# One decoder layer on one core: sums of W_down made in DRAM early, sums of x made on z between products

## The chip, the cores and the metric

The kernel runs on one core of one Trainium2 chip. The core has five engines that run their own instruction streams: TensorE (PE, matmuls; its weight loads are shown as PEld), VectorE (DVE), ScalarE (ACT), GpSimd (POOL) and SyncE (SP, which here only issues DMAs), and 16 DMA engines that serve all queues. The metric is the device time of one launch in microseconds. Three runs of the kernel before gave 2015.41, 2019.3 and 2021.93 us, median 2019.3.

## The reference

One hybrid decoder layer on x of 512 tokens by 2048 (batch 1), all in float32:

```python
proj = jnp.einsum("bsd,de->bse", x, w_in[l])            # 2048 -> 1024+128+128+3*1024
q, k, v, gate_b, gate_c, h = jnp.split(proj, split_pts, axis=-1)
q, k = rope(q), rope(k)
attn = sliding_window_gqa(q, k, v, attn_sinks[l])       # 16 q heads, 2 kv heads, window 128
conv = gate_b * causal_depthwise_conv(gate_c * h, short_conv_w[l])
y = jnp.einsum("bsm,md->bsd", jnp.concatenate([attn, conv], axis=-1), w_out[l])
x = layer_norm(DEEPNORM_ALPHA * x + y, ln1_g[l], ln1_b[l])
u = causal_depthwise_conv(jnp.einsum("bsd,df->bsf", x, ffn_w_up[l]), ffn_conv_w[l])
a, g = jnp.split(u, 2, axis=-1)                         # 5632 each
y = jnp.einsum("bsf,fd->bsd", jax.nn.silu(a) * g, ffn_w_down[l])
x = layer_norm(DEEPNORM_ALPHA * x + y, ln2_g[l], ln2_b[l])
```

## The kernel before

**Numbers as pairs.** Every matmul operand is split into a high part (ScalarE casts it, L183) and a low part (VectorE subtracts the high part, L184). Each product is the sum of two or three matmuls of such parts, accumulated in PSUM. Each weight piece of 128 x 1024 thus costs one ScalarE and one VectorE instruction before TensorE can use it.

**Stages.** All weights lie in one DRAM tensor `ws` of 1 MB chunks in the order of use. SP loads them one after the other into `raw` buffers (`dma_to`).
1. Projections, 0 to about 372 us: the first q panel (512 columns), k and v, the second q panel, then the convolution's panels with the attention of 16 units between them. q and k are rotated in `rope`: VectorE makes two products, `wa` (L256) and `wb` (L259), two buffers of each, and POOL adds them into `qm` (L261). `att_q` (L310 to L313) later splits `qm` and transposes it on TensorE.
2. W_out and the first layer norm, to about 605 us. In `ln1` POOL adds the bias to z (L683).
3. Up stage, about 606 to 1517 us: x times W_up in 44 column pairs `f`, each by a Strassen–Winograd scheme of seven products. A product (f, p) is eight matmuls of L482 and eight of L484 and takes a weight piece and an operand x of its number. The operands 1, 2 and 4 are quarters of x (x11, x12 and x22: the first index the half of the tokens, the second the half of the columns); 5, 6, 3 and 7 are sums: x5 = x21 − x22, x6 = x5 − x11, x3 = x6 + x12, x7 = x11 − x21. `product_order` gives the order.
4. Down stage, about 1526 to 1962 us: ten blocks `n` of W_down by the same scheme, each product in two halves (L614 to L616), evacuated by VectorE into z (L630); then a tail with the second layer norm.

**x sums before.** `ln1_transpose` transposes z in groups of four (L694) into PSUM and splits three quarters into operands. `x_sums` (L415) then makes each sum by two VectorE adds of 128 x 512 per piece from the high and the low parts, and splits it again. It is called after the first product.

**W_down sums before.** Product 5 of a block takes the weight w3 + w0, then other sums follow in the same buffer `wqd`: `d_load` copies w3 from DRAM and adds w0 with two accumulating DMAs (L545, on POOL's queue), VectorE adds w2 ahead of product 6 (L566), POOL's DMA adds w1 after it. Product 7 takes w3 + w2, added onto the raw chunk of w3 by POOL's DMAs as it is loaded.

**What sets the order.** Each engine runs its list in order, which a scheduler has fixed before the launch; an instruction that waits on a semaphore holds all behind it on its engine. The weight piece of a product is split four products ahead (`prepare(i + 4)`). POOL's list has its DMAs and its adds in one order.

Of the kernel before, what the change touches and what calls it, by code (L numbers as in the profile page):

```python
# [57 lines left out]
def product_order():  # L58

    order = [(0, 1), (0, 2), (1, 1), (1, 2), (0, 5), (0, 6)]  # L60
    for f in range(1, NF + 1):
        block = [(f, 5), (f, 1), (f - 1, 7), (f - 1, 3), (f, 2), (f, 6), (f - 1, 4)]
        if f == NF - 1:
            block = [block[i] for i in (0, 1, 2, 3, 5, 4, 6)]
        order += [x for x in block if x[0] < NF and x not in order]
    return order


def down_order():
    order = [(0, 5)]  # L70
    for n in range(NB):
        order += [(n, 1), (n, 2), (n, 6), (n, 3), (n, 7)] + [(n + 1, 5)] * (n + 1 < NB) + [(n, 4)]
    return [(n, p, h) for n, p in order for h in range(2)]


def layout_weights(w_in, w_out, w_up, w_down):
# [19 lines left out]
    parts.append(up.reshape(NF, 2, 2, P, 1024).transpose(0, 1, 3, 2, 4).reshape(2 * NF, P, 2048))  # L96
# [21 lines left out]
class Kernel:  # L118
# [19 lines left out]
    def dma_to(self, c):  # L138
        nc = self.nc
        while self.next_dma <= min(c, NCHUNK - 1):  # L140
# [7 lines left out]
            for c1 in cuts:  # L148
                nc.sync.dma_start(t[:, c0:c1], self.ws_d[i][:, c0:c1])
# [6 lines left out]
            if C_UP <= i < C_DOWN and (i - C_UP) % 2:  # L156
                self.w_add(t[:, 1024:], (i - C_UP) // 2, 1, 0)
            if C_DOWN <= i < C_TAIL and (i - C_DOWN) % 4 == 3:
                for h in range(2):
                    self.d_add(t, (i - C_DOWN) // 4, 2, h)  # L160
# [252 lines left out]
    def x_sums(self, tb):  # L413

        tt = lambda o, a, b, op: self.nc.vector.tensor_tensor(o, a, b, op=op)  # L415
        tk = slice((tb % 2) * P, (tb % 2 + 1) * P)
        for q in range(2):
            k = slice(4 * q, 4 * q + 4)
            part = lambda i, a: self.xs[i][:, k, a, tk].bitcast(F32)
            put = lambda i, src: self.split(self.xs[i][:, k, 0, tk], self.xs[i][:, k, 1, tk], src)  # L420
            x21 = self.x21[tb, q]
            t = self.p_s.tile([P, 4, P], F32, name="s")
            for i, j, first, op in ((5, 4, x21, ALU.subtract), (6, 1, t, ALU.subtract), (3, 2, t, ALU.add)):
                tt(t, first, part(j, 0), op)
                tt(t, t, part(j, 1), op)
                put(i, t)
            t = self.p_s.tile([P, 4, P], F32, name="s")
            tt(t, part(1, 0), x21, ALU.subtract)
            tt(t, t, part(1, 1), ALU.add)
            put(7, t)  # L430

    def w_add(self, dst, f, i, j):

        self.nc.gpsimd.dma_start(dst, self.ws_d[C_UP + 2 * f + i][:, 1024 * j:1024 * (j + 1)], accum_op=ALU.add)  # L434

    def q_load(self, f):

        if f < NF:
            t = self.wq[f] = self.p_q.tile([P, 1024], F32, name="wq")
            self.nc.sync.dma_start(t, self.ws_d[C_UP + 2 * f + 1][:, 1024:])  # L440
            self.w_add(t, f, 0, 0)

    def up_raw(self, f, i):

        c = C_UP + 2 * f + i
# [3 lines left out]
    def up_prep(self, f, p):  # L449
# [9 lines left out]
        if p == 5:  # L459
            self.w_add(src, f, 1, 0)  # L460
        elif p == 6:
# [4 lines left out]
        elif p == 2:  # L466
            del self.raw[C_UP + 2 * f]
        elif p == 3:
            del self.raw[C_UP + 2 * f + 1]

    def up_mm(self, f, p):
# [5 lines left out]
        if new:  # L477
            self.bank[kind, f] = self.psum("mm" if kind == "a" or kind == "b" and f < 2 else "aux")
# [8 lines left out]
    def up_evac(self, f, p, ps):  # L487
# [39 lines left out]
    def up(self, a, b):  # L527

        for i in range(a, b):
# [3 lines left out]
            for j, what in ((1, 3), (1, 4), (2, 4)):  # L533
                if i >= j and self.order[i - j][1] == what:
# [3 lines left out]
                    else:  # L538
                        self.up_conv(g, 1 if what == 3 else 0)
# [6 lines left out]

    def d_load(self, n):

        if n < NB:
            t = self.wq[n] = self.p_qd.tile([P, 2048], F32, name="wqd")  # L550
            self.nc.gpsimd.dma_start(t, self.ws_d[C_DOWN + 4 * n + 3])
            for h in range(2):
                self.d_add(t, n, 0, h)

    def down_prep(self, n, p, h):
# [45 lines left out]
    def down_half(self, n, p, h):  # L601
# [4 lines left out]
        if new and h == 0:  # L606
            self.bank[kind, n] = [self.psum("mm" if kind == "a" else "aux") for _ in range(2)]
# [11 lines left out]
    def down_evac(self, n, p, ps):  # L619
# [5 lines left out]
        for b in range(2):  # L625
            z = self.z[2 * t + b][:, 1024 * a + 512 * c:1024 * a + 512 * (c + 1)]
# [5 lines left out]
    def down(self, hs, hi, lo, tb, cs):  # L632

        sl = slice(tb * P, (tb + 1) * P)
        ps = self.psum("aux")[:, :cs.stop - cs.start]
        for f, (hh, hl) in enumerate(hs):
            self.mm3(ps, hh[:, sl], hl[:, sl], hi[:, f, :], lo[:, f, :], f == 0, f == len(hs) - 1)
        z = self.z[tb][:, cs]
        self.nc.vector.tensor_tensor(z, z, ps, op=ALU.add)

    def tail(self, hs, places):
# [11 lines left out]
        for tb in range(NTB):  # L653
# [3 lines left out]
            for i, (c0, c1) in enumerate(cuts):  # L657
# [3 lines left out]
                nc.vector.bn_stats(stats[:, i, :], self.z[tb][:, c0:c1])  # L661
# [10 lines left out]
    def ln1(self, tb):  # L672
# [5 lines left out]
        for j in range(4):  # L678
            cs = slice(512 * j, 512 * (j + 1))
            z = self.z[tb][:, cs]  # L680
# [4 lines left out]
    def ln1_transpose(self, tb):  # L685

        nc = self.nc
        tk = slice((tb % 2) * P, (tb % 2 + 1) * P)
        for j in range(4):
            keep = tb >= 2 and j < 2  # L690
            ps = self.psum("mm" if tb >= 2 and j >= 2 else "aux").rearrange("p (k t) -> p k t", t=P)
            for k in range(4):
                kt = 4 * j + k
                nc.tensor.transpose(ps[:, k, :], self.z[tb][:, kt * P:(kt + 1) * P], self.ident)  # L694
            k = slice(4 * (j % 2), 4 * (j % 2) + 4)
            if keep:
                self.x21[tb, j] = ps
                continue
            x = self.xs[{(0, 0): 1, (0, 1): 2, (1, 1): 4}[tb // 2, j // 2]]
            self.split(x[:, k, 0, tk], x[:, k, 1, tk], ps)  # L700

    def ln2(self, tb, stats, last):
# [5 lines left out]
        zs = [self.z[tb][:, c] for c in cs]  # L708
# [14 lines left out]
    def run(self):  # L723
# [10 lines left out]
        self.ps = {"mm": opened("psmm", 4, space=psum), "aux": opened("psaux", 4, space=psum)}  # L734
# [9 lines left out]
        zd = [p_d.tile([P, D], F32, name=f"zd{tb}") for tb in range(NTB)]  # L744
# [62 lines left out]
        for i in range(2 * NC_CONV):  # L807
# [5 lines left out]
            self.feat_half(hi, lo, q, pss)  # L813
            if q == 3:
# [16 lines left out]
        cm_up = [self.pool(n, b, "left") for n, b in (("q", 3), ("m", 2), ("u2", 2), ("u", 1))]  # L831
# [14 lines left out]
        def z_evac(ps, tb, c0, n, si, first):  # L846
            z = self.z[tb][:, c0:c0 + n]
# [8 lines left out]
        for n in range(3):  # L856
            pss = [self.psum("aux" if n % 2 else "mm") for _ in range(NTB)]
            for h in range(8):
                self.tok_half(j + h, 2, 512, 2 * h, pss)
                if n == 0 and h == 7:  # L860
                    cm_mix.__exit__(None, None, None)
                    cm_gb, p_gb = self.pool("gb", 1, "right")
                    cm_z, p_z = self.pool("z", 1, "left")
                    z = p_z.tile([P, NTB, D], F32, name="z")
                    self.z = [z[:, tb, :] for tb in range(NTB)]
                    for tb in range(NTB):
                        nc.sync.dma_start(self.z[tb], self.x_d[tb * P:(tb + 1) * P, :])
# [13 lines left out]
        j += 4  # L881
        self.xs = {i: self.x_view(self.act[:, r, :]) for i, r in ((1, 0), (2, 1), (4, 2), (7, 3))}
        for tb in range(NTB):
# [6 lines left out]
            z_evac(ps, tb, 1792, 256, 4, True)  # L890
            if tb >= 2:
                self.ln1_transpose(tb - 2)
            self.ln1(tb)
        for tb in range(2, NTB):
            self.ln1_transpose(tb)
        for tb in range(NTB):
# [122 lines left out]
```

## Time and profile before

| what | us |
|---|---|
| median of three runs | 2019.3 |
| the profiled execution, device time | 2018.78 |
| its span | 2016.7 |
| PE busy | 1928.5 (96%) |
| DVE busy | 1405.6 (70%) |
| ACT busy | 918.8 (46%) |
| POOL busy | 286.3 (14%) |

The busy shares are means over stages with different limits. The page's slices show TensorE's granted clock at full speed nearly throughout, lower only around 600 to 650 us, and the DMA engines full in the up stage, about half used before. A wait is read with the engine that ended it: "PE mm L614 <- DVE z L630" is TensorE idle ahead of L614 until VectorE's L630 had written z. DMA shares are of 16 engines.

### The profile page before, as it was taken

The page shows a single profiled execution, that of the slowest core. Times are in us where ns is not written, and L with a number is a line of the kernel's source. Part 1 is how long each engine was busy: PE and PEld are TensorE (multiplying, and loading weights), DVE is VectorE, ACT ScalarE, POOL GpSimd, SP SyncE. Part 2 cuts the span into 40 slices and gives each one's busy share as a digit, 9 for nine tenths or more (in the row PEclk, how much of TensorE's full clock was granted, in tenths as well). Part 3 has the DMA queues.
Part 4 walks back from the last instruction along what each step waited for, and adds up shares of the span by engine and source line. Part 5 has one row for each costly group of instructions (what it writes and reads, how often), then busy time and mean ns, then how long its engine had stood idle before and what let it go on. Part 6 is the DMA issues. An engine that isn't in the chain of part 4 may idle for free. (4 is left out here: it accounts for less than half of the span.)

```text
span 2016.7 us, 25991 instructions
## 1 busy us (share of the span) xinstructions
PE 1928.5 (96%) x9950; PEld 1638.4 (81%) x9950; DVE 1405.6 (70%) x2001; ACT 918.8 (46%) x1403; POOL 286.3 (14%) x315
## 2 busy tenths in 40 slices
PE   9999999999994899999999999999997989999887
PEld 7988888888893788888888888888885778787766
DVE  5357676353358777777777777777777778787777
ACT  4234444232124555555555555555555544344331
POOL 1110000000033111111111111111111111111104
PEclk9999999999996999999999999999998999999989
DMA  6222122552234599999999999999998868888762
GB/s 264 101 88 84 63 84 75 156 219 94 105 110 130 145 263 253 266 240 263 250 258 259 243 261 248 262 246 258 255 238 238 247 194 242 220 233 245 237 188 84
DMA packets 93499, 398.73 MB, mean 198 GB/s; under 512 B 9472, under 2 KB 20768, under 8 KB 67520
## 3 DMA queue, kind: packets, MB, share of 16 engines
q0 software_dynamic: 36256, 139.11, 36.2%
q1 hardware_dynamic: 56544, 256.92, 34.2%
q8 instruction: 78, 1.28, 0.2%
q10 hardware_dynamic: 576, 1.05, 0.1%
q14 instruction: 45, 0.37, 0.0%
HBM read 377.12 MB, written 19.92 MB: 197 GB/s over the span
## 5 line engine op out<-in xcount | busy, mean ns | idle before, releaser
L184 DVE TENSOR_TENSOR wlo<-raw,whi 128x1024 fp32r<-128x1024 f32 (+1 forms) x358 | 438.2, 1227 | 293.2 <-ACT whi L183 292.8
L183 ACT CAST whi<-raw 128x1024 fp32r<-128x1024 f32 (+1 forms) x358 | 373.5, 1045 | 574.9 <-PE mm L216 118.3
L482 PE MATMUL mm<-act,whi 128*128 128x512 f32 x1072 | 385.0, 400 | 0.0
L484 PE MATMUL mm<-act,wlo 128*128 128x256 f32 x1072 | 302.1, 282 | 0.0
L482 PE MATMUL aux<-x,whi 128*128 128x512 f32 x704 | 252.7, 395 | 20.9 <-DVE x L184 20.0
L482 PEld LDWEIGHTS mm<-act,whi 128*128 128x128 f32 x1072 | 202.7, 189 | 49.7 <-DVE mt L490 0.2
L434 POOL DMA_DIRECT2D wq<-ws x132 | 129.5, 983 | 726.0 <-DVE wlo L184 605.7
L184 DVE TENSOR_TENSOR wlo<-wq,whi 128x1024 fp32r<-128x1024 f32 x132 | 161.1, 1223 | 98.6 <-ACT whi L183 98.4
L484 PEld LDWEIGHTS mm<-act,wlo 128*128 128x128 f32 x1072 | 204.0, 190 | 0.4 <-DVE wlo L184 0.3
L183 ACT CAST whi<-wq 128x1024 fp32r<-128x1024 f32 x132 | 138.2, 1050 | 139.4 <-PE mm L482 50.3
L484 PE MATMUL aux<-x,wlo 128*128 128x256 f32 x704 | 199.6, 284 | 0.0
L482 PEld LDWEIGHTS aux<-x,whi 128*128 128x128 f32 x704 | 133.1, 189 | 52.1 <-DVE x L184 20.3
L214 PE MATMUL mm<-act,whi 128*128 128x512 f32 x384 | 151.5, 394 | 0.0
L216 PE MATMUL mm<-act,wlo 128*128 128x512 f32 x384 | 150.1, 391 | 0.0
L215 PE MATMUL mm<-act,whi 128*128 128x512 f32 x384 | 149.6, 390 | 0.0
L484 PEld LDWEIGHTS aux<-x,wlo 128*128 128x128 f32 x704 | 133.2, 189 | 0.2
L482 PE MATMUL mm<-x,whi 128*128 128x512 f32 x352 | 125.5, 393 | 2.3 <-DVE m L490 1.2
L614 PE MATMUL mm<-whi,act 128*128 128x512 f32 x256 | 103.5, 405 | 21.4 <-DVE z L630 21.4
L482 PE MATMUL aux<-act,whi 128*128 128x512 f32 x336 | 120.4, 398 | 0.0
L214 PE MATMUL mm<-whi,act 128*128 128x512 f32 (+1 forms) x316 | 116.5, 369 | 0.0
L216 PE MATMUL mm<-whi,act 128*128 128x512 f32 (+1 forms) x316 | 116.2, 368 | 0.0
L215 PE MATMUL mm<-wlo,act 128*128 128x512 f32 (+1 forms) x316 | 116.2, 368 | 0.0
(202 smaller groups left out, 3837.0 us busy)
## 6 DMA issues: line engine op xcount, KB each, us to landing
raw<-ws SPq DMA_DIRECT2D x180, 1024.0 KB, 8.2
wq<-ws POOLq DMA_DIRECT2D x132, 512.0 KB, 9.3
raw<-ws POOLq DMA_DIRECT2D x64, 512.0 KB, 7.6
wq<-ws SPq DMA_DIRECT2D x44, 512.0 KB, 8.2
wqd<-ws POOLq DMA_DIRECT2D x40, 512.0 KB, 13.2
hd<-ca SPq DMA_DIRECT2D x44, 256.0 KB, 10.0
h<-hd SPq DMA_DIRECT2D x22, 512.0 KB, 12.8
wqd<-ws POOLq DMA_DIRECT2D x10, 1024.0 KB, 5.1
```

Source lines behind the costliest of these rows:

```text
L183: self.nc.scalar.copy(hi, src)
L184: self.nc.vector.tensor_tensor(lo, src, hi.bitcast(F32), op=ALU.subtract)
L214: mm(ps, sh, mh, start=start, stop=False)
L215: mm(ps, sh, ml, start=False, stop=False)
L216: mm(ps, sl, mh, start=False, stop=stop)
L434: self.nc.gpsimd.dma_start(dst, self.ws_d[C_UP + 2 * f + i][:, 1024 * j:1024 * (j + 1)], accum_op=ALU.add)
L482: mm(ps, hi[:, sl], x[:, k, :, :].rearrange("p a t -> p (a t)"), start=new and k == 0, stop=False, skip_group_check=not new)
L484: mm(ps[:, :H], lo[:, sl], x[:, k, 0, :], start=False, stop=k == 7, skip_group_check=not new)
L614: mm(ps[b], xh, hi[:, k, :], start=new and h == 0 and k == 0, stop=False, **kw)
```

## The change

Three parts. In the feed-forward's down stage the sums w3 + w0 and w3 + w2 of every block are made in DRAM tensors (`sums`) by `w_sum`: one DRAM-to-DRAM copy of 1 MB and two accumulating DMAs of 512 KB each, 20 sums in all, on POOL's queue; the down stage loads them as they are, w2 is added to `wqd` by POOL's DMAs after product 5, and L566 goes. In the up stage the first six products are 1 and 2 of three column pairs, then 5 of two; between them VectorE makes the sums of x in place on z (8 adds of 128 x 1024 in place of 32 of 128 x 512), and TensorE transposes each result (28 groups of four in place of 16). In `ln1` two of the last block's four bias adds go from POOL to VectorE, and z is written to DRAM (`zd`) by eight DMAs on POOL's queue in place of four on SP's. PSUM's second pool is split in two from the up stage on, and z is held in tiles that are freed one by one.

```diff
 def product_order():
-    order = [(0, 1), (0, 2), (1, 1), (1, 2), (0, 5), (0, 6)]
+    order = [(f, p) for f in range(3) for p in (1, 2)] + [(0, 5), (1, 5)]
     for f in range(1, NF + 1):
         block = [(f, 5), (f, 1), (f - 1, 7), (f - 1, 3), (f, 2), (f, 6), (f - 1, 4)]
+        if f == 1:
+            block = [(0, 6), (1, 6), (0, 7), (0, 3), (0, 4)]
...
+    def x_sum(self, tb, p):
+        tt = self.nc.vector.tensor_tensor
+        (a11, a12), (a21, a22) = self.z[tb - 2], self.z[tb]
+        dst, x, y, op = {5: (a22, a21, a22, ALU.subtract), 7: (a21, a11, a21, ALU.subtract),
+                         6: (a22, a22, a11, ALU.subtract), 3: (a22, a22, a12, ALU.add)}[p]
+        tt(dst, x, y, op=op)
...
+    def w_sum(self, k):
+        s = k // 2 if k % 2 == 0 else (k - 3) // 2
+        if not 0 <= s < 2 * NB:
+            return
+        n, p = s // 2, (5, 7)[s % 2]
+        w = lambda i: self.ws_d[C_DOWN + 4 * n + i]
+        if k % 2 == 0:
+            self.nc.gpsimd.dma_start(self.sums[n, p], w(3))
+        else:
+            for h in range(2):
+                c = slice(1024 * h, 1024 * (h + 1))
+                self.nc.gpsimd.dma_start(self.sums[n, p][:, c], w(0 if p == 5 else 2)[:, c], accum_op=ALU.add)
     def d_load(self, n):
         if n < NB:
             t = self.wq[n] = self.p_qd.tile([P, 2048], F32, name="wqd")
-            self.nc.gpsimd.dma_start(t, self.ws_d[C_DOWN + 4 * n + 3])
-            for h in range(2):
-                self.d_add(t, n, 0, h)
+            self.nc.gpsimd.dma_start(t, self.sums[n, 5])
...
-        if p == 6:
-            self.nc.vector.tensor_tensor(src[:, cs], src[:, cs], self.raw[C_DOWN + 4 * n + 2][:, cs], op=ALU.add)
         self.split(hi, lo, src[:, cs])
         self.hl[n, p, h] = (hi, lo)
-        if p == 6:
+        if p == 5:
+            self.d_add(src, n, 2, h)
+        elif p == 6:
             self.d_add(src, n, 1, h)
...
-            nc.gpsimd.tensor_tensor(z, z, self.gb[:, 1, cs], op=ALU.add)
+            e = nc.vector if tb == 3 and j % 2 else nc.gpsimd
+            e.tensor_tensor(z, z, self.gb[:, 1, cs], op=ALU.add)
+        for c in range(2):
+            nc.gpsimd.dma_start(self.zd[tb][:, 1024 * c:1024 * (c + 1)], self.z[tb][c])
...
             self.feat_half(hi, lo, q, pss)
+            self.w_sum(i - 2)
...
         self.up(0, 1)
-        for tb in range(2, NTB):
-            self.x_sums(tb)
-        self.up(1, 20)
+        self.x_tr(2, 1, 4, "bc")
+        self.x_sum(2, 5)
+        self.up(1, 3)
+        self.x_tr(2, 1, 5, "bc")
+        self.x_sum(2, 7)
+        self.up(3, 4)
...
-        last = self.order.index((NF - 1, 6)) + 1
+        last = self.order.index((NF - 1, 3)) + 1
```

Where the instructions come to stand: first POOL from its last small load (`fcw`) on, at the kernel's start. Before, the rotated q (`qm`, L261) and k (`kr`) follow at once:

```order
L777 DMA fcw<-fcw 128x264
L261 TENSOR_TENSOR qm_169<-wa,wb 128x512
L261 TENSOR_TENSOR qm_170<-wa,wb 128x512
L261 TENSOR_TENSOR qm_171<-wa,wb 128x512
L261 TENSOR_TENSOR qm_172<-wa,wb 128x512
L261 TENSOR_TENSOR kr<-wa,wb 128x128 x4
```

With the change, the sums (`sum_5_106` is w3 + w0 of block 0, `sum_7_107` w3 + w2 of it, and so on; L577 is the copy, L581 an accumulating DMA, L268 the rotation's add):

```order
L804 DMA fcw<-fcw 128x264
L577 DMA sum_5_106<-ws 16x16384
L577 DMA sum_7_107<-ws 16x16384
L581 DMA sum_5_106<-ws 128x1024 x2
L577 DMA sum_5_108<-ws 16x16384
L581 DMA sum_7_107<-ws 128x1024 x2
L577 DMA sum_7_109<-ws 16x16384
L581 DMA sum_5_108<-ws 128x1024 x2
L577 DMA sum_5_110<-ws 16x16384
L581 DMA sum_7_109<-ws 128x1024 x2
L577 DMA sum_7_111<-ws 16x16384
L581 DMA sum_5_110<-ws 128x1024 x2
```

The sums stand ahead of the first rotation's adds, each pair of accumulating DMAs behind a copy that it must wait for.

Second, POOL further on in the changed kernel, where the second q panel's adds stand (`qm_189` is token block 0):

```order
L577 DMA sum_5_120<-ws 16x16384
L581 DMA sum_7_119<-ws 128x1024 x2
L577 DMA sum_7_121<-ws 16x16384
L581 DMA sum_5_120<-ws 128x1024 x2
L577 DMA sum_5_122<-ws 16x16384
L581 DMA sum_7_121<-ws 128x1024
L268 TENSOR_TENSOR qm_189<-wa,wb 128x512
L268 TENSOR_TENSOR qm_190<-wa,wb 128x512
L581 DMA sum_7_121<-ws 128x1024
L577 DMA sum_7_123<-ws 16x16384
L268 TENSOR_TENSOR qm_191<-wa,wb 128x512
```

Sixteen of the 20 sums' copies are ahead of one that an instruction in front of `qm_189` waits for; before, this add had only the first panel's and k's adds ahead of it.

Third, VectorE at the start of the up stage. Before, the sums of x (`s`, L415) follow each other, with splits (L184) and evacuations (L490) between them:

```order
L415 TENSOR_TENSOR s_5073<-aux_4962,act_88 128x512
L415 TENSOR_TENSOR s_5086<-act_88,aux_4962 128x512
L415 TENSOR_TENSOR s_5073<-s_5073,act_88 128x512
L415 TENSOR_TENSOR s_5086<-s_5086,act_88 128x512
L490 TENSOR_TENSOR m1_5194<-mm_5177,m1_5194 128x256
L184 TENSOR_TENSOR wlo_5173<-wq_5028,whi_5172 128x1024
L184 TENSOR_TENSOR x5_5023<-s_5073,x5_5023 128x4x128
```

With the change (L426 is a sum in place on z, L191 a split, L508 an evacuation):

```order
L191 TENSOR_TENSOR act_88<-b_5121,act_88 128x4x128
L191 TENSOR_TENSOR act_88<-c_5126,act_88 128x4x128
L426 TENSOR_TENSOR z21_3967<-z20_3974,z21_3967 128x1024
L191 TENSOR_TENSOR wlo_5137<-raw_4606,whi_5136 128x1024
L508 TENSOR_TENSOR mt_5157<-b_5140,mt_5157 128x256
L191 TENSOR_TENSOR wlo_5163<-raw_4606,whi_5162 128x1024
L508 TENSOR_TENSOR ua_5160<-m1_5118,mt_5157 128x256
L508 TENSOR_TENSOR m1_5183<-mm_5166,m1_5183 128x256
L191 TENSOR_TENSOR x5_5075<-b_5186,x5_5075 128x4x128
```

One sum of a whole half row takes the place of several, and weight splits of the first products stand between it and the split of its result.

## Rows read from the trace of the kernel before

**Rows 1.** Waits of TensorE: line, waited for; us in total, times, longest us.

```profile
PE mm L614 <- DVE z L630: 25.4, 8, 7.3
PE aux L482 <- DVE x L184: 20.0, 1, 20.0
PE aux L614 <- ACT whi L183: 10.0, 2, 9.4
```

**Rows 2.** Windows: length, busy us of each engine, granted clock, DMA share, GB/s.

```profile
core 0: us, PE busy (x) PEld busy (x) DVE busy (x) ACT busy (x) POOL busy (x), PEclk, DMA share, GB/s
...
640.00:660.00 20.00, 2.42 (x7) 2.13 (x8) 20.00 (x34) 6.41 (x12) 1.59 (x2) 0.52 0.34 53
...
606.00:700.00 94.00, 60.26 (x312) 50.13 (x311) 72.60 (x107) 41.41 (x66) 20.83 (x18) 0.80 0.51 130
700.00:1500.00 800.00, 800.00 (x4546) 697.58 (x4545) 617.41 (x898) 447.57 (x694) 141.65 (x161) 1.00 1.00 254
...
1540.00:1950.00 410.00, 381.47 (x1623) 308.88 (x1621) 322.93 (x340) 180.88 (x187) 54.92 (x66) 0.98 0.81 232
```

**Rows 3.** Windows at the kernel's start, columns as in rows 2.

```profile
5.00:35.00 30.00, 29.26 (x128) 23.72 (x127) 19.19 (x26) 17.89 (x27) 0.16 (x1) 1.00 0.95 381
...
5.00:117.00 112.00, 111.26 (x587) 95.53 (x586) 48.90 (x81) 37.21 (x56) 9.01 (x9) 1.00 0.44 168
```

**Rows 4.** Windows of L482 alone: length, PE busy (x), PEld busy (x).

```profile
606.00:700.00 94.00, 50.72 (x136) 26.77 (x137) 0.80 0.51 130
...
720.00:800.00 80.00, 80.00 (x228) 42.66 (x228) 1.00 1.01 263
```

**Rows 5.** Timeline of TensorE, transposes of z: start us, us.

```profile
604.96 1.91 PE L694 MATMUL aux<-ident,z 128*128 128x128 f32 x16
```

**Rows 6.** VectorE's groups, 604 to 700 us: busy us, mean ns | idle before.

```profile
L415 DVE TENSOR_TENSOR s<-s,act 128x512 f32<-128x512 f32 x24 | 15.2, 682 | 0.0
...
L184 DVE TENSOR_TENSOR x<-s,x 128x512 fp32r<-128x512 f32 x12 | 7.9, 683 | 0.1
L681 DVE SCALAR_TENSOR_TENSOR z<-z,mv,gb 128x512 f32<-128x512 f32 x6 | 6.3, 1098 | 0.0
```

**Rows 7.** Timeline of VectorE in the down stage: start us, us, [idle before].

```profile
1656.09 2.36 DVE L566 TENSOR_TENSOR wqd<-wqd,raw 128x1024 f32<-128x1024 f32 x2 [7.13 <-DMA raw<-ws]
1658.37 1.22 DVE L184 TENSOR_TENSOR wlo<-wqd,whi 128x1024 fp32r<-128x1024 f32 x1
```

**Rows 8.** Timelines of POOL and TensorE at the down stage's start.

```profile
1515.08 1.82 POOL L545 DMA_DIRECT2D wqd<-ws  x2 [7.58 <-DMA wqd<-ws]
...
1526.47 0.80 PE L614 MATMUL aux<-whi,act 128*128 128x512 f32 x1 [9.36 <-ACT whi L183]
```

**Rows 9.** Waits of VectorE at L566.

```profile
DVE wqd L566 <- DMA raw<-ws: 27.4, 5, 7.9
```

**Rows 10.** Timeline of TensorE in the down stage.

```profile
1660.33 0.48 PE L614 MATMUL mm<-whi,x 128*128 128x512 f32 x1 [3.98 <-DVE z L630]
...
1871.57 0.47 PE L614 MATMUL mm<-whi,act 128*128 128x512 f32 x1 [3.35 <-DVE z L630]
...
1953.43 0.77 PE L614 MATMUL mm<-whi,act 128*128 128x512 f32 x1 [7.28 <-DVE z L630]
```

**Rows 11.** Waits of POOL, whole kernel.

```profile
POOL raw L434 <- DMA raw<-ws: 252.2, 20, 145.3
```

**Rows 12.** DMA queues from 720 to 1400 us: packets, MB, share of 16 engines.

```profile
q0 software_dynamic: 20080, 73.12, 60.8%
q1 hardware_dynamic: 19821, 98.94, 38.7%
```

**Rows 13.** DMA issues, whole kernel: KB each, median us to landing.

```profile
zd<-z SPq DMA_DIRECT2D x4, 1024.0 KB, 4.4
```

**Rows 14.** Timeline of POOL: the second q panel's adds.

```profile
117.40 2.56 POOL L261 TENSOR_TENSOR qm<-wa,wb 128x512 f32<-128x512 f32 x2 [38.54 <-DVE wb L259]
```

**Rows 15.** Timelines of VectorE and TensorE behind them.

```profile
118.74 0.69 DVE L256 TENSOR_TENSOR wa<-mm,rope_t 128x512 f32<-128x512 f32 x1 [0.15 <-POOL qm L261]
...
123.64 0.46 PE L313 MATMUL aux<-identr,qs 128*128 128x128 f32 x4
```

More of the change, by code (lines that the diff above doesn't have):

```diff
@@ L411, in x_view, with x_tp, x_split, x_tr @@
         return tile.rearrange("p (k a t) -> p k a t", a=2, t=H)
-    def x_sums(self, tb):
-        tt = lambda o, a, b, op: self.nc.vector.tensor_tensor(o, a, b, op=op)
-        tk = slice((tb % 2) * P, (tb % 2 + 1) * P)
[L417 to L430, printed above, removed]
+    def x_sum(self, tb, p):
[4 more added lines that the diff above has]
+        tt(dst, x, y, op=op)
+    def x_tp(self, tb, c, kinds="bb"):
+        pss = []
+        for g in range(2):
+            ps = self.psum(kinds[g]).rearrange("p (k t) -> p k t", t=P)
+            for i in range(4):
+                kt = 4 * g + i
+                self.nc.tensor.transpose(ps[:, i, :], self.z[tb][c][:, kt * P:(kt + 1) * P], self.ident)
+            pss.append(ps)
+        return pss
+    def x_split(self, tb, p, pss):
+        tk = slice((tb % 2) * P, (tb % 2 + 1) * P)
+        for g, ps in enumerate(pss):
+            k = slice(4 * g, 4 * g + 4)
+            self.split(self.xs[p][:, k, 0, tk], self.xs[p][:, k, 1, tk], ps)
+    def x_tr(self, tb, c, p, kinds="bb"):
+        self.x_split(tb, p, self.x_tp(tb, c, kinds))
     def w_add(self, dst, f, i, j):
-        self.nc.gpsimd.dma_start(dst, self.ws_d[C_UP + 2 * f + i][:, 1024 * j:1024 * (j + 1)], accum_op=ALU.add)
+        self.nc.gpsimd.dma_start(dst, self.ws_d[C_UP + UP_PIECES[2 * f + i]][:, 1024 * j:1024 * (j + 1)], accum_op=ALU.add)
     def q_load(self, f):
@@ L679, in ln1, with zc @@
             cs = slice(512 * j, 512 * (j + 1))
-            z = self.z[tb][:, cs]
+            z = self.zc(tb, cs.start, cs.stop)
             nc.vector.scalar_tensor_tensor(z, z, mv[:, 0:1], self.gb[:, 0, cs], op0=ALU.subtract, op1=ALU.mult)
             nc.scalar.activation(z, z, AF.Copy, scale=r)
-            nc.gpsimd.tensor_tensor(z, z, self.gb[:, 1, cs], op=ALU.add)
[L685 to L700, printed above, removed]
+            e = nc.vector if tb == 3 and j % 2 else nc.gpsimd
+            e.tensor_tensor(z, z, self.gb[:, 1, cs], op=ALU.add)
+        for c in range(2):
+            nc.gpsimd.dma_start(self.zd[tb][:, 1024 * c:1024 * (c + 1)], self.z[tb][c])
+    def zc(self, tb, c0, c1):
+        w = D // len(self.z[tb])
+        return self.z[tb][c0 // w][:, c0 % w:c0 % w + c1 - c0]
     def ln2(self, tb, stats, last):
@@ L707, in ln2 @@
         cs = [slice(512 * j, 512 * (j + 1)) for j in range(4)]
-        zs = [self.z[tb][:, c] for c in cs]
+        zs = [self.zc(tb, c.start, c.stop) for c in cs]
         for j in (0, 2, 1, 3) if last else range(4):
@@ L743, in run @@
         self.hd = [p_d.tile([P, 4, S], F32, name=f"hd{u}") for u in range(ND)]
-        zd = [p_d.tile([P, D], F32, name=f"zd{tb}") for tb in range(NTB)]
+        self.zd = zd = [p_d.tile([P, D], F32, name=f"zd{tb}") for tb in range(NTB)]
+        self.sums = {(n, p): p_d.tile([P, D], F32, name=f"sum{n}_{p}") for n in range(NB) for p in (5, 7)}
         self.x_at, self.xraw = 0, {}
@@ L830, in run @@
         cm_e.__exit__(None, None, None)
-        cm_up = [self.pool(n, b, "left") for n, b in (("q", 3), ("m", 2), ("u2", 2), ("u", 1))]
+        cm_up = [self.pool(n, b, "left") for n, b in (("q", 3), ("m", 2), ("u2", 3), ("u", 1))]
         self.p_q, self.p_m, self.p_u2, self.p_u = (p for _, p in cm_up)
```

144 lines of the change are left out of this document (89 added, 55 removed).

## The prediction

> **What bounds the kernel now.** I first read the waits of TensorE, since TensorE is busy nearly throughout and a change is worth what it takes from or adds to its idle time. Three lines carry most of that [rows 1]: the down stage's products wait 25.4 us for sums that VectorE writes into z (L630), the up stage waits once for 20.0 us for a split of x (L184), and the start of the down stage waits 9.4 us for a cast of W_down. Then I read the windows around these [rows 2]. From 606 to 700 us TensorE works 60.26 us of 94.00 at a mean granted clock of 0.80; from 640 to 660 us it works 2.42 us while VectorE is busy for all 20.00; from 700 to 1500 us it does not pause. So the start of the up stage is bound by VectorE, its body by TensorE, and the down stage (381.47 of 410.00) by TensorE with short waits. Last I read the start of the kernel for what is to be added there: TensorE is busy for 111.26 of 112.00 us between 5 and 117 us, with the DMA engines at a share of 0.44 [rows 3]. That stretch has spare DMA time, but the same rows show that none of it lies ahead of 35 us, where the share is 0.95.
>
> **Start of the up stage: x sums.** A product is eight matmuls of L482 with eight of L484. There are 136 of L482 from 606 to 700 us, so 17 products, and 228 in the 80 us from 720 us, so 28.5, 2.81 us each [rows 4]. Seventeen cost 47.7 us. Twelve groups of four transposes fall into the stretch too; 16 of them take 1.91 us when nothing holds them [rows 5], 0.48 us a group, 5.8 us. So 94 − 47.7 − 5.8 = 40.5 us are lost there, 33.7 as idle time and some 7 to the lower of the two clock levels behind the waits.
>
> The change keeps 28 splits of 512 elements, but makes the sums with 8 adds of 1024 elements in place of 32 of 512, and adds 12 groups of transposes (5.8 us of TensorE). On VectorE an add of 512 costs 15.2/24 = 0.63 us, a split of 512 7.9/12 = 0.66 [rows 6], an operation of 1024 1.14 (the next starts 2.28 us after a pair) [rows 7]. Per add of 1024 it does twice the work in 1.8 times the time, so 32 × 0.63 = 20.2 us become 8 × 1.14 = 9.1. More is gained by order: VectorE makes x5 for one token block while TensorE already has two, then three, column pairs' products 1 and 2 to do. Up to x6 ready VectorE has 20 splits (13.2), 10 weight splits (11.4), the sums (9.1) and about 9 of ln1 and evacuations (of which the ln1 passes are 6.3 [rows 6]), 43 us, so until about 605 + 43 = 648. TensorE has eight products (22.5) and 18 groups (8.6) till then, and must wait about 5 us at the first split of block 1. That leaves another 5 us of waiting, and I add 3 for the gaps between groups and the clock behind them: 5.8 + 5.8 + 47.7 + 5 + 5 + 3 = 72 us for what took 94. Gain 22 us, between 14 (VectorE's chain waits for each transpose group) and 30 (it never holds TensorE).
>
> **Start of the down stage.** TensorE waits 9.36 us at 1526.47, because POOL issued the two adds of the first sum at 1515.08, after waiting 7.58 us for the copy to land [rows 8]. The change loads a finished sum, so one landing goes. But the pool opens a product later than before (four products left, not five), which gives back 2.8 us, and the h tiles are to be loaded as well. I take a gain of 4 us, between a loss of 3 and a gain of 9 (the whole wait).
>
> **Down stage.** L566, 20 adds of 1.14 us, disappears; five times it waits for its raw chunk, 7.9 us at most [rows 9]. At 1656.09 it waited 7.13 us [rows 7] and held up the evacuations behind it on VectorE, and TensorE's wait of 3.98 at 1660.33 follows. There are four such, the last of 3.35 at 1871.57 [rows 10], 15.8 us together; for the lower clock behind them (a first matmul of 0.77 us at 1953.43 against 0.48 elsewhere [rows 10]) I allow 2 us in all. Of the 7.28 us at 1953.43 I count 3, as part of it is the tail's own chain. The DMAs that replace L566 (w2 added into wqd by POOL after product 5) have the products 1 and 2 to land beside. Gain 21 us, between 10 and 27 (all of the 25.4 and the clock).
>
> Together 22 + 4 + 21 = 47 us gained, between 30 and 62.
>
> **The sums of W_down in DRAM.** They are 20 copies of 1 MB and 20 pairs of 512 KB accumulating DMAs, all on POOL's queue, and by the order of POOL's instructions they begin right behind fcw, at about 5 us, not in the conv loop where the source has them. POOL waits for a copy before its pair. So the rope adds stand behind them: the first of the first q panel can't run before the fifth copy has landed (some 3 pairs are through by then), the first of the second q panel not before the sixteenth, with some 14 pairs through (the fifteenth is issued just ahead). That POOL really stands still for a landed load is to be seen in before: L434's `raw` waited 252.2 us for 20 of them [rows 11].
>
> No row shows a DRAM-to-DRAM copy. The nearest row is a plain transfer in a full stretch: q1 moved 98.94 MB in 38.7% of 680 us, 2.66 us per MB, 2.8 for 1024 KB [rows 12]. A write of 1 MB to DRAM landed in 4.4 us [rows 13], no slower than loads, which speaks for the same price. Accumulating transfers were nearly all of q0: 73.12 MB in 60.8%, 5.65 us per MB, 5.9 per pair [rows 12]. Sixteen copies cost 45 us and 14 pairs 83 us, all engines. The loads that the weights need till 117 us took 0.44 × 112 = 49 us [rows 3]; I take 44 of them, since loads of the last 10 us serve later panels. So the first rope add of the second q panel comes at about 5 + 45 + 83 + 44 = 177 us, instead of 117.40 [rows 14].
>
> What waits for it: VectorE. It has two wa/wb buffers, so its rope of block 2 waited already for POOL's add of block 0 (at 118.74 [rows 15]) by 0.15 us. Behind that instruction stand VectorE's splits of the next weights, and TensorE's first attention transposes need qs at 123.64 [rows 15]. TensorE can go on with the products whose weights are split, a few us, so nearly the whole delay of 60 us arrives, 57. It isn't won back: the panels around it keep TensorE busy without a gap [rows 3], so there is nothing to catch up with. The slowing of the first loads (35 us of share 0.95 against POOL's queue) lies inside this, because it lets the same target come at the same time. The last 4 copies run beside conv panels and cost nothing.
>
> The lower end of the loss: if both kinds cost what an undisturbed packet does (381 GB/s at share 0.95 [rows 3], so 2.6 per copy, and the accumulating one twice that, 5.2, since it also reads its target), the add comes at 5 + 42 + 73 + 40 = 160, a loss of 41. If an accumulating DMA cost as a plain one (16 × 2.8 + 14 × 2.8 + 44 + 5 = 133), 14 us; rows 12 speak against that. Upper end: a copy that pays for reading and for writing DRAM, 5.2 to 5.6 each, adds 38 to 45 us, a loss of 95 to 102. I take 57, as plain transfer and accumulation each have a row.
>
> No row here can show what a copy costs. The Trainium skill (DMA: Bandwidth & Descriptors, section Latency and other measured facts) gives 207 to 214 GB/s per direction for DMA copies from one HBM tensor to another. By that a copy of 1024 KB would take 4.9 to 5.1 us, an estimate from that page, and the sum would be some 34 us later, near 2063.
>
> **The sum.** 2018.78 (the profiled execution; span 2016.7) − 47 + 57 = 2028.8, and as the median of the runs is 0.5 us above that execution, 2029 to 2030. I say 2030.
>
> **Rivals.**
> *The sums stay hidden (faster).* If POOL's queue interleaves well, an accumulation costs less alone than in the saturated stretch (where share 1.00 may hold waiting as well as work), and POOL reaches the rope adds no more than 0 to 35 us late. It decides from a pair price of 5.0 us down: 5 + 45 + 14 × 5.0 + 44 = 164, a loss of 47, as much as is gained. For it: TensorE did not wait at all in that stretch, though the DMA share was 1.00 [rows 2], so the prices may be inflated; and the order itself places rope adds among the DMAs as if they were nearly in time. Against: the first 30 us have no spare share. Time: 2019 − 47 + (0 to 35), 1972 to 2007, about 1992.
> *Copies pay for both sides (much slower).* A loss of 95, 2018.8 − 47 + 95 = 2067. For it: each byte crosses DRAM twice. Against: the 4.4 us of a written MB.
> *The x part fails (slower, one mechanism).* VectorE's in-place chain on z is serial: each sum may only start when the transposes of the former content are done, and each transposition only when the sum is; if at every one of the eight steps TensorE waits a VectorE queue position (a weight split and an evacuation, about 1.5 us, and the low clock behind), 12 us and 8 more of the 22 go: the up stage gains 2 and the whole is 2018.8 − 27 + 57 = 2049. It decides if the chain's total passes 605 + 43 + 15 = 663 us.
> *The change does not do what it says there:* the scheduler's order is static, so that it would put the sums beside the conv panels at run time is excluded by the order; this has no share.
>
> **How the numbers follow.** Differences under 0.3% (6 us) can't be told from none. Forecast 2030 (2014 to 2045): 0.40. Hidden sums: 0.32. Copies at both sides: 0.16. The x part fails: 0.12. Faster by over 0.3% (below 2013): the hidden case, of which 0.29, and 0.03 of the forecast's lower end, 0.32. Within 0.3% (2013 to 2025): 0.14, from the forecast's lower half with the loss near 41 to 50 and the hidden case's upper end. Slower: 0.54. The range for 8 in 10 leaves one tenth below 1985 (all gains with a loss under 15) and one above 2070.
>
> **What would show it.** In the profile after: rope adds of the second q panel (L268) near 177 us rather than 117 and preceded by POOL waits for `sum` DMAs; TensorE idle for some 57 us between 50 and 190 us, and its clock low behind; 606 to 700 us (moved along) with 17 products in about 72 us; L566 gone and no TensorE wait of 4 us on z in mid stage. I am wrong if POOL's rope adds come by 125 us, if TensorE has its wait within the first 45 us (then the loads in the head set it, not the queue), or if the 606 to 700 stretch still shows one wait of over 10 us.

## The result, and the profile after

The changed kernel takes 2045.26 us (median; 2043.8 to 2047.12) against 2017.36 for the kernel before in the same rounds: a ratio of 1.0131, interval 1.0113 to 1.0149. It is slower, as forecast, but by 28 us and not by 11, and just above the forecast's range of 2014 to 2045. The profiled execution has a span of 2042.3 us, 25.6 more than before.

First the waits of TensorE in the profile after (line, waited for; us in total, times, longest us), which answer to [rows 1]:

```profile
PE aux L320 <- DVE qs L317: 33.2, 1, 33.2
PE mm L221 <- ACT act L190: 20.8, 5, 6.4
PE mm L500 <- DVE act L191: 6.7, 1, 6.7
PE b L435 <- DVE x L191: 5.1, 1, 5.1
PE mm L648 <- ACT x L190: 5.1, 1, 5.1
...
PE mm L648 <- DVE z L664: 3.3, 1, 3.3
```

The 25.4 us behind z in the down stage are 3.3, and the 20.0 us wait for x is gone. In their place stand two things of the kernel's start: 33.2 us at the first attention transposes (L320) and five waits for splits of the input x (L221 behind L190). POOL's timeline shows the first of these (start us, us, [idle before]):

```profile
5.17 1.02 POOL L577 DMA_DIRECT2D sum<-ws  x2
14.14 1.76 POOL L581 DMA_DIRECT2D sum<-ws  x2 [7.96 <-DMA sum<-ws]
...
31.82 1.64 POOL L581 DMA_DIRECT2D sum<-ws  x2 [12.59 <-DMA sum<-ws]
...
175.97 1.64 POOL L581 DMA_DIRECT2D sum<-ws  x2 [6.22 <-DMA sum<-ws]
177.02 1.09 POOL L577 DMA_DIRECT2D sum<-ws  x1
184.00 0.80 POOL L581 DMA_DIRECT2D sum<-ws  x1 [5.88 <-DMA sum<-ws]
184.55 2.75 POOL L268 TENSOR_TENSOR qm<-wa,wb 128x512 f32<-128x512 f32 x2
```

The last line answers to [rows 14]: the second q panel's first rotation add starts at 184.55 us instead of 117.40, straight behind a wait of 5.88 us for a sum's copy. What stands behind it on VectorE and TensorE answers to [rows 15]:

```profile
186.12 0.69 DVE L263 TENSOR_TENSOR wa<-mm,rope_t 128x512 f32<-128x512 f32 x1 [31.41 <-POOL qm L268]
```

```profile
191.43 0.75 PE L320 MATMUL aux<-identr,qs 128*128 128x128 f32 x4 [33.21 <-DVE qs L317]
```

VectorE waited 31.41 us for POOL where it waited 0.15 before, and TensorE reached its first attention transposes at 191.43 instead of 123.64: 67.8 us late. Windows of the profile after (columns as in [rows 2]):

```profile
0.00:80.00 80.00, 56.02 (x187) 40.33 (x188) 22.61 (x30) 21.59 (x30) 16.50 (x32) 0.86 0.98 309
80.00:158.00 78.00, 78.00 (x441) 68.26 (x439) 30.77 (x57) 18.56 (x30) 23.02 (x30) 0.99 0.98 272
158.00:191.40 33.40, 0.22 (x1) 0.00 (x0) 5.28 (x8) 1.04 (x1) 13.44 (x16) 0.54 1.02 258
666.20:769.20 103.00, 83.95 (x499) 73.17 (x498) 83.22 (x115) 55.49 (x89) 32.52 (x32) 0.92 0.68 175
...
1607.00:1986.60 379.60, 374.62 (x1642) 308.19 (x1641) 304.75 (x320) 183.54 (x186) 38.15 (x48) 1.00 0.79 224
```

The same stretches of the kernel before:

```profile
0.00:80.00 80.00, 78.06 (x425) 66.23 (x426) 39.57 (x72) 30.37 (x48) 13.42 (x23) 1.00 0.51 194
597.00:700.00 103.00, 69.25 (x390) 59.13 (x389) 80.55 (x119) 49.02 (x78) 28.38 (x24) 0.82 0.51 136
```

```profile
1545.40:1961.10 415.70, 387.77 (x1639) 314.25 (x1640) 325.59 (x342) 182.59 (x188) 54.92 (x66) 0.97 0.80 231
```

The loss comes in two halves. The first is done when VectorE starts the second q panel's rope products, at 150.37 us instead of 115.97. Up to there TensorE ran the same 590 matmuls; first after, then before:

```profile
0.00:150.00 150.00, 126.02 (x589) 102.13 (x590) 49.55 (x79) 38.31 (x57) 39.43 (x61) 0.92 0.98 290
```

```profile
0.00:116.00 116.00, 114.06 (x590) 96.00 (x591) 48.17 (x80) 38.49 (x57) 13.42 (x23) 1.00 0.45 169
```

It was idle for 24.0 us instead of 1.9, and the same matmuls took 12.0 us longer at a mean granted clock of 0.92 instead of 1.00: 34 us. The second half is the 33 us at L320.

Of the gains, the up stage's start (103 us from the first transposes of z) gives 499 matmuls instead of 390; of them 167 of L500 against 136 of L482, 3.9 products of 2.81 us, less what is missing in the records, some 10 us. The down stage's body has the same 1640 matmuls in 379.6 us instead of 415.7, 36 us less. How late the changed kernel is can be followed on TensorE's timelines from place to place:

| place | before | after | late by |
|---|---|---|---|
| first attention transposes | 123.6 | 191.4 | 67.8 |
| first transposes of z | 597.5 | 666.7 | 69.2 |
| products of the up stage done | 1519.9 | 1580.7 | 60.8 |
| start of the down stage's windows above | 1545.4 | 1607.0 | 61.6 |
| end of these windows | 1961.1 | 1986.6 | 25.5 |
| end of the span | 2016.7 | 2042.3 | 25.6 |

(Before, all but one product of the up stage were done at 1517.1, ahead of the wait of 9.36 us; the last one ran behind it and is counted with its 2.8 us.) So the up stage gave 8.4 us in all, 2.1 of its 10 being lost in a wait at 1577.62. The seam between the two stages gave nothing and took 0.8: TensorE now waits 5.1, 3.6 and 4.1 us there, where it waited 9.4 and 4.0. The first two are for ScalarE's splits of h, the down stage's other operand, which wait for its loads, while the casts of the finished sum had long been done (the first at 1573.06):

```profile
1584.72 1.04 ACT L190 CAST x<-h 128x1024 fp32r<-128x1024 f32 x1 [3.07 <-DMA h<-hd]
```

The down stage's body gave 36.1.

### The profile page after: what moved, and what is told of

The parts are those of the page before. It is cut to its first block, busy times and chain, and to the rows that moved or that the text cites. A ratio compares the mean times of both kernels' runs of the same rounds, so it can differ in the third digit from the quotient of the medians.

```text
span 2042.3 us, 26061 instructions
## 1 busy us (share of the span) xinstructions
PE 1935.0 (95%) x9998; PEld 1645.7 (81%) x9998; DVE 1383.6 (68%) x1959; ACT 921.3 (45%) x1403; POOL 308.8 (15%) x361
## 5 line engine op out<-in xcount | busy, mean ns | idle before, releaser
L191 DVE TENSOR_TENSOR wlo<-raw,whi 128x1024 fp32r<-128x1024 f32 (+1 forms) x358 | 437.3, 1223 | 292.8 <-ACT whi L190 292.4
L190 ACT CAST whi<-raw 128x1024 fp32r<-128x1024 f32 (+1 forms) x358 | 373.4, 1045 | 536.3 <-PE mm L222 107.5
L500 PE MATMUL mm<-act,whi 128*128 128x512 f32 x1056 | 379.3, 400 | 8.9 <-DVE act L191 6.7
L502 PE MATMUL mm<-act,wlo 128*128 128x256 f32 x1056 | 297.3, 282 | 0.0
L500 PE MATMUL c<-x,whi 128*128 128x512 f32 x704 | 250.8, 393 | 0.0
L500 PEld LDWEIGHTS mm<-act,whi 128*128 128x128 f32 x1056 | 199.2, 189 | 58.4 <-DVE act L191 7.0
L191 DVE TENSOR_TENSOR wlo<-wq,whi 128x1024 fp32r<-128x1024 f32 x132 | 161.3, 1223 | 83.5 <-ACT whi L190 83.3
L502 PE MATMUL c<-x,wlo 128*128 128x256 f32 x704 | 199.0, 283 | 0.0
L190 ACT CAST whi<-wq 128x1024 fp32r<-128x1024 f32 x132 | 138.5, 1050 | 133.8 <-PE c L500 51.3
L500 PEld LDWEIGHTS c<-x,whi 128*128 128x128 f32 x704 | 132.2, 188 | 30.3
L221 PE MATMUL mm<-act,whi 128*128 128x512 f32 x384 | 152.0, 396 | 0.0
L221 PE MATMUL mm<-whi,act 128*128 128x512 f32 (+1 forms) x316 | 120.8, 382 | 21.9 <-ACT act L190 20.8
L502 PEld LDWEIGHTS c<-x,wlo 128*128 128x128 f32 x704 | 132.3, 188 | 0.0
L500 PE MATMUL b<-act,whi 128*128 128x512 f32 x352 | 128.5, 404 | 1.5 <-DVE act L191 1.5
L500 PE MATMUL mm<-x,whi 128*128 128x512 f32 x352 | 125.3, 393 | 0.0
L223 PE MATMUL mm<-whi,act 128*128 128x512 f32 (+1 forms) x316 | 119.3, 377 | 0.0
```

The source lines that it names most:

```text
L190: self.nc.scalar.copy(hi, src)
L191: self.nc.vector.tensor_tensor(lo, src, hi.bitcast(F32), op=ALU.subtract)
L221: mm(ps, sh, mh, start=start, stop=False)
L223: mm(ps, sl, mh, start=False, stop=stop)
L500: mm(ps, hi[:, sl], x[:, k, :, :].rearrange("p a t -> p (a t)"), start=new and k == 0, stop=False, skip_group_check=not new)
L502: mm(ps[:, :H], lo[:, sl], x[:, k, 0, :], start=False, stop=k == 7, skip_group_check=not new)
```

## The experiments

Ratios are to the kernel before in the same rounds.

**late: the sums later.** A tile written behind the second q panel's rotation is put into each sum by a DMA of 4 bytes before its copy, so no sum can start before.

```diff
         self.q_evac(pss, 1)
+        self.gate = p_const.tile([P, 1], F32, name="gate")
+        nc.vector.tensor_copy(self.gate, self.qm[3][:, AW - 1:AW])
...
+            self.nc.gpsimd.dma_start(self.sums[n, p][0:1, 0:1], self.gate[0:1, :])
             self.nc.gpsimd.dma_start(self.sums[n, p], w(3))
```

> All of the change, but every sum of W_down is made to wait for the second q panel's rotation (a 4-byte DMA from a tile that VectorE writes behind it precedes each copy), so POOL's rotation adds stand ahead of all sums. Theory (the loss is the sums' place: they hold POOL's queue and the rings before 190 us, and cost nothing beside the convolution's panels): the 67.8 us delay at the first attention transposes goes, the gains of 42 us at the up and down stages stay: 1975 us, within 8. Rival (the sums cost DMA time wherever they stand, and slow the loads of the panels): at least 20 us of waits of TensorE between 130 and 400 us, 1995 or more. Second rival (the gains came only because the later stages were better fed after the early waits): 2005 to 2017.

1975.52 us, ratio 0.9782 (0.9763 to 0.9801): faster than both kernels. The first attention transposes start at 123.6 us. A window of late, with the sums in the rings:

```profile
200.00:300.00 100.00, 100.00 (x520) 84.59 (x519) 68.75 (x147) 50.05 (x130) 24.47 (x36) 1.00 1.00 265
```

TensorE has no idle time there at a DMA share of 1.00. From its first attention transposes to the first transposes of z it takes 473.5 us, as long as before (473.8). So the sums' DMA time as such costs nothing beside the panels; both rivals fall, and the loss is the place. The span of late, 1973.7 us, is 43.0 below that of the kernel before: the gains of the table above (8.4 − 0.8 + 36.1 = 43.7) without the loss. Repeated in a later batch (late_b):

> The kernel late again, beside late_noadd on the same chip: 1975 us, within 3.

1975.52 again, 0.9797 (0.9784 to 0.9811).

**rope_dve: the rotation's adds off POOL's queue.**

```diff
-        nc.gpsimd.tensor_tensor(dst, t1, t2, op=ALU.add)
+        nc.vector.tensor_tensor(dst, t1, t2, op=ALU.add)
```

> The changed kernel with the rotation's adds on VectorE instead of POOL; the sums stay at the start. Theory (the loss of 67.8 us is two things: about 34 us by slow loads in the first 80 us, and 33 us at L320 by POOL's queue): only the second goes, 2045 - 33 + 1 for the adds on VectorE = 2013 us, TensorE idle 24 us before 80 us as now and no wait over 5 us at the first attention transposes. Rival (the rings are what delays all, POOL's queue only shows it): the loads of the second q panel and of the panels behind come late too, and TensorE waits elsewhere between 80 and 230 us by 15 us or more, 2028 or more.

2009.05 us, 0.9947 (0.9928 to 0.9967), 36 us less than the changed kernel (33 in the spans). Its waits of TensorE:

```profile
PE mm L221 <- ACT act L190: 16.2, 5, 4.2
PE mm L648 <- ACT x L190: 8.2, 1, 8.2
```

The 33 us at L320 are gone and the waits in the head stay (the clock of the first 80 us is 0.86 again); the transposes come at 157.3 us:

```profile
L320 PE MATMUL aux<-identr,qs x64: 221/238/253, 157.3 to 360.7; 128*128 128x128 f32 x64
```

So 34 us of the 67.8 stay with the slow loads when POOL's order is out of the way, and 34 go with it.

**copies and plain: what a sum costs the rings.** copies leaves the accumulating DMAs out, plain makes them plain ones; the down stage then works with other weights.

```diff
-                self.nc.gpsimd.dma_start(self.sums[n, p][:, c], w(0 if p == 5 else 2)[:, c], accum_op=ALU.add)
+                self.nc.gpsimd.dma_start(self.sums[n, p][:, c], w(0 if p == 5 else 2)[:, c])   # plain
```

> The changed kernel with the 20 copies alone: the accumulating DMAs of the sums are left out (so products 5 and 7 of the down stage use w3 in place of the sums). Theory (ring time: 2.8 us a copy, 5.9 a pair): 20 copies cost 56 us, with the loads' 51 done by 112 us, so the second q panel's add comes at 117 to 125 us, and only the first loads are slowed, by 10 to 25 us: 1985 to 2002 us. Rival (a copy pays for reading and for writing, 5 us): 100 us of copies, the add near 150, 2010 us or more.

> The changed kernel with the sums' 40 accumulating DMAs made plain copies of the same shape (so the sums hold w0 or w2 alone). Theory (ring time, 3.0 us per MB copy, and the same for a plain pair in place of 5.2): the second q panel's add at 5 + 16 x 3.0 + 15 x 3.0 + 51 = 149 us, when the panel itself is only just done because of the slow first loads: TensorE's wait of 33 us at L320 goes, the head's 34 us stay, 2010 us (2004 to 2016). Rival (landings in turn, copy then pair, set POOL's pace, not ring time): the add stays near 170 or later and 2028 or more.

copies: 2011.85 us, 0.9958 (0.9945 to 0.997). The time is the rival's, the price is not. The queues of copies from 5 to 150 us (packets, MB, share of 16 engines), and two of its waits:

```profile
q0 software_dynamic: 896, 21.65, 41.3%
q1 hardware_dynamic: 3500, 17.89, 33.2%
```

```profile
26.86 0.80 PE L221 MATMUL mm<-whi,act 128*128 128x512 f32 x1 [12.01 <-ACT whi L190]
51.57 0.80 PE L221 MATMUL mm<-whi,act 128*128 128x512 f32 x1 [18.99 <-ACT act L190]
```

A share of 41.3% of 145 us is 59.9 us for 20 copies, 2.9 to 3.0 each. (The Trainium skill, DMA: Bandwidth & Descriptors, section Latency and other measured facts, gives 207 to 214 GB/s per direction for copies of 128 x 16 KiB tiles between HBM tensors on the sync and scalar queues; by that, an estimate, a copy would take 4.9 to 5.1 us. These copies have another shape, 16 rows, and go by POOL's queue; here it was 21.65 MB in 59.9 us of all engines, 361 GB/s, and the measurement decides.) But with nothing to wait for, POOL has put 8 copies into the rings by 12 us, beside the loads of x, which landed 39.3 us after their issue (median) instead of 9.6:

```profile
xraw<-xt SPq DMA_DIRECT2D x6, 512.0 KB, 39.3
```

The second q panel's add comes at 153.82 us and waits for VectorE, not for a DMA, and the first attention transposes come at 160.1. So copies alone cost 36 us in the head; my theory had 10 to 25, and its 1985 to 2002 us were missed.

plain: 2007.41 us, 0.9954 (0.993 to 0.9977). POOL's add:

```profile
146.46 2.49 POOL L268 TENSOR_TENSOR qm<-wa,wb 128x512 f32<-128x512 f32 x2
```

149 was expected by ring time. Halving the adds' price moves the add from 184.55 to 146.46 with the same number of landings in turn, so the pace followed the rings' time and not the number of POOL's landings. The whole time came out as expected, its two parts did not: the head costs less than with the adds (9.7 us of waits for splits of x instead of 20.8), and 8.1 us of the wait at L320, which was to go, are left.

**mid: the sums behind the first q panel only.** As late, with the gate tile taken from the first panel.

> The changed kernel with the sums made to wait for the first q panel's rotation only: in POOL's order the four first rotation adds then stand ahead of all sums, and nine copies and eight pairs ahead of the second panel's first add. Theory (rings full until the add may run; 3.0 us a copy and 5.2 a pair as in copies and late): from 56 us, 9 x 3.0 + 8 x 5.2 + 20 us of loads + 5 to 10 of landings of the small DMAs, the add near 150 us instead of 117, no wait of TensorE before 60 us, one of about 25 to 33 at the first attention transposes: 2000 to 2009 us. Rival (the slow first loads are what costs, a late queue is made good): under 1990.

2000.1 us, 0.9911 (0.9891 to 0.9932).

```profile
PE aux L320 <- DVE qs L317: 21.5, 1, 21.5
```

The head is undisturbed, the second panel's add comes at 141.83 us and TensorE waits 21.5 us, less than the 25 to 33 expected. So the loads' part (rope_dve) and the queue's part (here) can each be had alone; the queue's part is smaller here than in the changed kernel, with fewer sums ahead of the add.

**xpart and downonly: the parts alone.** xpart takes the sums in DRAM out of the change (L566 and the accumulating loads are back). downonly puts them, at late's place, into the kernel before, and leaves its x sums, product order and opening of the buffers.

> The x part alone: no sums in DRAM; the down stage's weights are summed as in the kernel before (L566 on VectorE, accumulating DMAs). Theory: the up stage's start gives 20 us by itself and the down part the other 22, so 1997 us (1990 to 2003), with TensorE's four waits of 3 to 5 us on z in the down stage back. Rival: the up stage's gain is smaller without the down part (or the order of products at its end costs): 2005 or more.

> The kernel before with the W_down sums alone, placed after the second q panel as in the run late; the up stage's start, the product order and the place where the down stage's buffers are opened stay as before. Theory (from late: 35 us of its 44 are the down stage's waits and the lower clock behind them, 10 are the x part, and the stage seam gives nothing): 1984 us (1979 to 1989), with TensorE idle under 8 us between the seam and the end of the down stage. Rival (the forecast's terms, x part 22 and down part 21): 1996 or more.

xpart: 2019.87 us, 1.0004 (0.9989 to 1.0019): nothing gained, 23 us off what I expected. Its waits:

```profile
PE mm L651 <- DVE z L667: 26.3, 9, 8.5
PE c L651 <- ACT act L191: 16.1, 1, 16.1
```

The up stage ends earlier (its last product at 1510.7 us), but TensorE then stands 16.1 us until 1527.33, where it stood 9.4 before: the down stage's buffers open a product later. What TensorE waits for there is not the sum, whose casts stand at 1516.29 and 1517.87, but ScalarE's splits of h, the down stage's other operand, which wait for its loads, 8.64 us at 1515.34 and then:

```profile
1525.02 1.04 ACT L191 CAST x<-h 128x1024 fp32r<-128x1024 f32 x1 [6.12 <-DMA h<-hd]
```

Why the loads of h take longer here was not measured; the copy and its adds are in the rings beside them. With the sums ready (late) two waits are in its place, 4.9 and 3.6 us. The rest of xpart's lost gain is the head, 2 us later than in late, and the up start's, which was smaller than I thought.

downonly: 1981.23 us, 0.9819 (0.9802 to 0.9836), as expected from late's stages. Its down stage (the window starts some ten matmuls further on than those above):

```profile
1546.00:1921.60 375.60, 373.05 (x1629) 306.91 (x1628) 303.79 (x318) 182.14 (x185) 38.62 (x48) 0.99 0.80 227
```

So the down part alone is worth 35 us, and the x part adds some 6 to it (1981.23 to 1975.52; 4 to 7 by the ratios, as the two were not run in the same rounds). With the buffers opened as before, the finished sums do gain at the seam: the wait of 4.03 us for a low part of W_down ends at 1542.03 instead of 1545.39, 3.4 us earlier.

**late_noadd: why the up stage's start gave 10 us.** One accumulating DMA is left out, so that one product uses another's weight. In late ScalarE's list has the cast of product (0, 6)'s weight ahead of the splits of x5 (first fence), and TensorE's two longest waits there are 6.71 us for the first splits of block 1 and 7.00 at x5's (second fence):

```profile
644.91 1.04 ACT L190 CAST whi<-wq 128x1024 fp32r<-128x1024 f32 x1 [8.57 <-DMA wq<-ws]
645.86 0.58 ACT L190 CAST x<-b 128x512 fp32r<-128x512 f32 x1
```

```profile
616.15 0.80 PE L500 MATMUL mm<-act,whi 128*128 128x512 f32 x1 [6.71 <-DVE act L191]
...
647.22 1.12 PE L435 MATMUL b<-ident,z 128*128 128x128 f32 x4 [7.00 <-DVE x L191]
```

```diff
         if p == 5:
-            self.w_add(src, f, 1, 0)
+            if f:
+                self.w_add(src, f, 1, 0)
```

> The kernel late without one transfer: the accumulating DMA of 512 KB that adds onto wq between the products (0, 5) and (0, 6) is left out (so product (0, 6) uses the weight of (0, 5)). ScalarE's cast of that weight stands ahead of the splits of x5 in its list, and in late it waits 8.57 us for this DMA, TensorE 7.0 us behind it at 647 us. Theory (the x part's gain came out at 10 instead of 22 us mostly because this transfer, not VectorE's chain, holds the x splits there): the 7.0 us wait goes to under 2 and the lower clock behind it, 6 to 10 us less than late in the same batch. Rival (VectorE's chain of sums and splits is as long as that itself): within 3 us of late.

1971.77 us, 0.9772 (0.9759 to 0.9786), 3.75 us less than late_b. The wait of ScalarE is gone:

```profile
636.46 1.04 ACT L190 CAST whi<-wq 128x1024 fp32r<-128x1024 f32 x1 [1.06 <-issue]
```

TensorE's wait of 5 to 7 us at 647 us is gone with it. But the time lies between theory and rival (the intervals of the ratios of late_noadd and late_b overlap at their ends), and the up stage ends only 3 us earlier. So this transfer holds some 3 to 4 of the 12 us that the up stage's start gave less than forecast; how the rest divides was not measured by a run.

## Why the prediction was wrong

The direction, the mechanism and nearly every place were right; the difference of two large terms was too small by 16 us (10 against 25.6 in the spans), because all four forecasts in it were mis-sized: the loss (57 forecast, 67.8 to 69.2 measured), the up stage's start (22; 8.4 to 10), the seam (4; −0.8) and the down stage (21; 36.1).

*The sums at POOL's start.* The step "5 + 45 + 83 + 44 = 177" stood at 184.55. The queues of the profile after from 5 to 184 us say which term was off:

```profile
q0 software_dynamic: 4904, 32.55, 70.8%
q1 hardware_dynamic: 3642, 18.93, 28.5%
```

POOL's queue took 70.8% of 179 us, 127 us, where I had 128: right as a sum, by small errors that cancel. Its 32.55 MB are 0.7 of small loads (2 us), 16 copies (2.9 us each instead of 2.8) and some 14.4 pairs (by the rest, 5.4 us instead of 5.9). The loads took 28.5%, 51 us, where I took 44. This is the step that failed: I had struck off the loads that serve later panels, but the queue moved 18.93 MB by then, 2.7 us each, and 44 us stand for 16.3; a load that had been issued took its time in the rings whether it was needed yet or not. That is 7 us. The next step, "nearly the whole delay of 60 us arrives, 57", was wrong by 3 more: the delay of the add, 67.2 us, arrived whole (67.8), as the transposes come 6.9 us behind the add and came 6.2 behind it before.

I also called the slow first loads part of the same target, and so they are, but rope_dve shows that they are half of the loss and would stay if POOL's order were mended. My sign of being wrong, a wait of TensorE within the first 45 us, came half true: it idled 10.9 us there, 42.8 from 50 to 190. That the idle time up to L320, 57.2 us, is the 57 of the forecast is luck: my 57 was the whole delay, and the measured one has some 12 us of lower clock besides, which I had not priced.

*The up stage's start.* 22 us forecast, 10 measured, of which 8.4 were left at the stage's end. The mis-sized term is the 13 us (5 + 5 + 3) that I gave to waits and low clock after the change. In late, 597 to 660 us, TensorE idles 20.9 us (2.3 and 6.7 at the first splits of block 1 where I had 5, 3.2 for the sums, 7.0 at x5's and 1.5 behind them) and runs at 0.74 to 0.86 of its clock in two of the three windows. One step that failed is the view that only VectorE's chain of 43 us sets this start: VectorE had written the last sum of x5 by 638.1 us, but its split goes through ScalarE's list, which waited for a DMA until 644.91. By late_noadd that is 3 to 4 us; the cause of the other 8 stays open.

*The seam.* 4 us forecast; it took 0.8. Finished sums remove a landing, as I said: that gave 3.4 us in downonly, where the buffers open as before. The term that failed is the later opening, for which I gave back 2.8 us and named the loads of h without a price. Between downonly and the changed kernel it cost about 4 (3.4 + 0.8), as TensorE then waits for h's loads.

*The down stage.* 21 us forecast, 36 measured, outside my bounds of 10 to 27. I counted four waits, 15.8 us, and 2 us of clock. The windows give 28 us idle before and 5 after, 23 where I had 19, and the rest, some 13 us, lies in TensorE's lower clock and slower matmuls behind the waits (granted 0.97 over 415.7 us, now 1.00). The term for the clock was the one mis-sized, 13 instead of 2: behind the waits, about half their length was lost again.

So the gains sum to 43.7 instead of 47, by errors of opposite sign, and that is luck; the loss is 68 to 69 instead of 57. Of the rivals, "copies pay for both sides" (2067) and "the x part fails" (2049) lay near in time, but the first is refuted by copies (2.9 us and not 5.2 to 5.6), and the second is wrong in its cause, as the up stage gained 8 us and not 2 and the loss was not 57; "the sums stay hidden" fell for this order and is true of late's.

## What to carry to other kernels

Work that nobody waits for still has a place: an engine's list in order and shared DMA rings make it an obstacle for all that is issued after it, so give early, independent DMAs a dependency that puts them where the rings have time to spare (before, their share was 0.31 from 124 to 597 us; here 70 us lie between the two places, 1975.52 and 2045.26). When the forecast is a difference of two terms five times its size, say how sure each term is and widen the range by both. And price a short wait of TensorE with the low clock behind it, read from the window's granted clock, not with its idle time alone.

## What the runs showed that was not expected

DRAM-to-DRAM copies of 1 MB in 16 rows cost the rings hardly more than loads do (2.9 us against 2.8). Accumulating into DRAM costs twice that, 5.5 to 5.7 us per 1 MB, little less than accumulating into the on-chip buffers beside full loads (5.9). This is read where POOL's queue has all 20 sums, 40 MB, from 5 to 240 us in the changed kernel and from 120 to 360 us in late:

```profile
q0 software_dynamic: 6656, 42.63, 72.2%
```

```profile
q0 software_dynamic: 7038, 41.95, 72.0%
```

That is 170 and 173 us; less 2 us for small loads in the first, and less 20 copies of 2.9, 110 and 115 us are left for 20 pairs.

Copies that wait for nothing are the worse neighbours: 20 of them without the adds delayed the loads of x to 39.3 us from issue to landing, with the adds between them to 32.4, against 9.6 alone.
